# Working-layout inputs and state-space tables kept in DRAM, in a hybrid diffusion block

## The chip, the cores and the metric

The kernel runs on one core of one Trainium2 chip. The metric is the device time of one execution in microseconds. The kernel before was timed in three runs: 2078.35, 2061.95 and 2072.16 us, median 2072.16. Its profile is that of one further execution.

## The reference

One layer of a diffusion backbone, in float32. Tokens: 256 context tokens (`ctx`) and 256 latent tokens (`x`), 2048 channels each. A modulation vector `silu(c) @ w_mod + b_mod` (2048 by 12288, for `c` and for `c_ctx`) gives shifts and scales; `h = x * (1 + scale) + shift` goes through one input projection `w_in` (2048 by 12304), whose columns feed three branches: a Hyena long convolution, a bidirectional mLSTM, and a bidirectional S5 state-space model. The three results are projected, gated, summed and go through `w_out`; then a layer norm, a squared-ReLU feed-forward part (2048 by 8192 and back) and a second layer norm.

What the change touches is mostly the S5 branch. It has 48 groups of 16 channels with 64 complex states each, for two directions:

```
dt = exp(log_dt);  ab = exp(dt * a)            (complex, per group and state)
bb = (ab - 1) / a * b                          (64 x 16 per group)
s[t] = ab * s[t-1] + bb @ u[t]                 (context first, then latent)
y[t] = Re(c @ s[t]);  both directions added, then d * u, gelu and a gated unit
```

## The kernel before

**Streams of weights.** Most of the time TensorE multiplies streamed weights. A chunk of 512 KB is loaded on SyncE's queue into a tile `wr`, split by ScalarE into a high part `wh` (L145) and by VectorE into the rest `wl` (L149), and multiplied in three products per pair of operands (high by high, high by low, low by high; L166, output tile `mm`). One chunk on the latent tokens alone is 24 matmuls of 128x256. Chunks of a column block follow each other over k; between chunks, `chunk_done` (L171) lets side generators advance by a rate. The order of instructions on each engine is then set by a planner, which goes through the traced order as a priority and takes what its own cost model holds to be ready; on the chip every engine runs its list strictly in that order. Tiles come from pools with few buffers, and a pool opened later reuses the memory of a closed one, so its first writers wait for the last readers there.

**First stage, phase 0** (`phase0`, L1476; 0 to about 200 us). For four groups of 512 channels: two blocks of the modulation (`mod_block`, L359, 8 chunks each, matmul L371 on PSUM tile `px`), then `h_load` and `h_group` (L383, L394): the tokens arrive with tokens on partitions, TensorE transposes them (L169, 64 in all), VectorE applies scale and shift (L407) and the result is split (`t`, L145 and L149). Among the next group's chunks run the key columns of the input projection. A side generator, started at the third group at rate 1.5, computes the S5 parameters (`s5_params`, L411: parameter rows are loaded with (direction, pair) on partitions and transposed by TensorE in `expand`), small vectors (`col_load`, `conv_cols`: loaded as rows, transposed, evacuated) and the lag kernels (`s5_lags`, L542: `s5_q`, L527, makes C times the powers of ab with six instructions per direction, forward on VectorE and backward on GpSimd, L535 to L540; 192 small matmul records at L564; result to DRAM as `KK`). At its end the powers and B go to DRAM as `SP`, C and the eighth power as `SC`. All of this lives in the scope `p0a`; its memory is next used by the scope `pA` (keys, values, mLSTM).

**The S5 stage** (scope `pB`, L1582 to L1592; 546 to about 1000 us). `SP` and `SC` have been read back. The stream is 36 chunks of the Hyena columns, then 96 chunks of the gate columns `mg`, of which 32 are traced before the output, 48 beside it, and the rest later. After 6 chunks comes the injection (`s5_inject`, L620): for each of 6 channel tiles, 12 instructions make B times the powers (L645 to L650, half of them on VectorE, half on GpSimd, tiles `s5q`, `z`, `s5tp`), 16 transposes (L169), four evacuations to `z`, 64 matmul records (L663), and evacuations into `S` by ScalarE and VectorE (L668). Then the scan (`s5_scan`, L671, side at rate 2): 63 steps of four GpSimd instructions (L678 to L681) on all of `S`. Then the output (`s5_output`, L684, side at rate 0.6): for each channel tile `s5_q` again makes C times the powers (12 instructions), the states are laid out (`b`, L145 and L707), 32 and 16 matmul records (L714, L720), 16 more to put them in place, and the sum into `z` (L729). `s5_glu` closes the branch.

Of the kernel before, what the change touches and what calls it, by code (L numbers as in the profile page):

```python
# [65 lines left out]

class Tiles(list):
    """Tiles by k, read as one operand [:, k, columns]."""
# [6 lines left out]
class Kern:  # L75
# [15 lines left out]
    # ---------------------------------------------------------------- helpers  # L91
# [4 lines left out]
    def c(self, name, rows=P):  # L96
        o, n = CN[name]
        return self.consts[:rows, o:o + n]

# [25 lines left out]
    def aux(self, shape, tag=None):  # L125
        """A PSUM bank: px for what the stream of weights waits on, aux for side work; in turn where both are free."""
# [44 lines left out]
    def chunk_done(self):  # L171
        """Lets side work be traced between the chunks of the stream of weights."""
# [18 lines left out]
    # weights stationary: out [cols on partitions, tokens]  # L191
    def lin_w(self, w, c0, ncols, kt, xs):
        """A block of columns; returns its PSUM tile [128, slots, 256] and a step function over k."""
# [5 lines left out]
        def step(k0, alone=False):  # L199
            """The products of nk k; with alone, not added to others."""  # L200
# [19 lines left out]
    def lin_w_steps(self, w, c0, ncols, kt, xs, consume):  # L220
        """Yields between the chunks."""
# [51 lines left out]
    def slices(self, buf, view=None, **dims):  # L273
        """Named temporaries out of one tile."""
# [9 lines left out]
    def exp_acc(self, out, x, tmp):  # L284
        """exp in float32 accuracy; tmp(tag, dtype) gives tiles of x's shape."""
# [28 lines left out]
    def rstd(self, var, shape, tag):  # L314
        """1 / sqrt(var + eps)"""
# [11 lines left out]
    def col_load(self, src, n, tag, at=0):  # L327
        """A vector of n*128 in DRAM as columns [128, n]."""
        rows = self.t(self.sm, [96, P], "rows", 2)[:n]
        self.nc.gpsimd.dma_start(rows, src.rearrange("(r p) -> r p", p=P))  # L330
        ps = self.aux([P, n])
        self.tr(ps, rows, n)
        col = self.t(self.cst, [P, n], tag)
        self.act(col, ps)
        return col

    # ---------------------------------------------------------------- phases
    def setup(self):
# [3 lines left out]
        crow = self.t(self.sm, [32, P], "crow", 1)  # L342
        nc.sync.dma_start(crow[:16], I["c"].rearrange("b (r p) -> (b r) p", p=P))
        nc.sync.dma_start(crow[16:], I["c_ctx"].rearrange("(r p) -> r p", p=P))
        ps = self.aux([P, 32])
        self.tr(ps, crow, 32)
        self.sc = self.t(self.cst, [P, 32], "sc")
        self.act(self.sc, ps, AF.Silu)
# [3 lines left out]
        self.bmod = self.col_load(I["b_mod"][0], 96, "bmod")  # L352
        nc.vector.tensor_scalar(self.bmod[:, 16:32], self.bmod[:, 16:32], 1.0, None, op0=ALU.add)
        nc.vector.tensor_scalar(self.bmod[:, 64:80], self.bmod[:, 64:80], 1.0, None, op0=ALU.add)
        self.modc = self.t(self.cst, [P, 32, 2], "modc")
# [27 lines left out]
    def h_load(self, g):  # L383
        nc = self.nc
        raws = []
        for s, src in enumerate((self.I["ctx"][0], self.I["x"][0])):
            src = src[:, g * 512:(g + 1) * 512]
            raw = [self.room[2 * s + tb][:, 4:6, :].rearrange("p k t -> p (k t)") for tb in range(2)]
            for tb in range(2):
                nc.sync.dma_start(raw[tb], src[tb * P:(tb + 1) * P])  # L390
            raws.append(raw)
# [1248 lines left out]
```

## Time and profile before

| what | value |
|---|---|
| median of three runs | 2072.16 us |
| span of the profiled execution | 2066.5 us |
| instructions | 34948 |
| PE busy | 1908.3 us (92%) |
| DVE busy | 1373.0 us (66%) |
| ACT busy | 799.8 us (39%) |
| POOL busy | 526.1 us (25%) |
| DMA moved | 435.64 MB, mean 211 GB/s |

The profile lists the span from the first to the last instruction, 2066.5 us, and no separate total for that execution; the median of the three runs is 5.7 us above it. PE is TensorE, DVE VectorE, ACT ScalarE, POOL GpSimd and SP SyncE, which here only issues loads. Busy PE time is modelled from pipelined instructions, so a stretch with PE at 100% can still go slower than another. The granted clock stands as a share of full speed.

### The profile page before, as it was taken

Reading aid. Unit: us, or ns where it says so; the run is one execution under the profiler, and the core shown is the slowest. Engines: PE = TensorE matmul, PEld = TensorE weight load, DVE = VectorE, ACT = ScalarE, POOL = GpSimd, SP = SyncE. Lnnn points to the kernel's source line nnn. Section 1 sums busy time; section 2 is a strip of 40 time slices with the busy share of each in tenths; the row PEclk is TensorE's granted clock in tenths of the full one; section 3 lists DMA queues with packets and bytes.
Section 4 is the critical chain, followed back from the end, with each engine's and each line's share of the span. In section 5 each row is a group of like instructions: output and inputs, shape, how many; then the busy total and the mean of one; then the engine's idle time right before and its main releaser. Section 6 shows DMA issues by size and latency. Waiting matters only on the chain.

```text
span 2066.5 us, 34948 instructions
## 1 busy us (share of the span) xinstructions
PE 1908.3 (92%) x14085; PEld 1733.0 (84%) x14085; DVE 1373.0 (66%) x1840; ACT 799.8 (39%) x1066; POOL 526.1 (25%) x656
## 2 busy tenths in 40 slices
PE   6889999999888999589988999799999999999995
PEld 2657988989888898579878978799989899998985
DVE  5567877547989855495688766966665555555556
ACT  1323333236444333234433443544443334444331
POOL 3435211000435799960243410500000000000001
PEclk7889999999999999789999999999999999999998
DMA  9777676766666676447766776577776666667663
GB/s 303 244 246 255 200 230 221 228 183 193 219 193 192 209 243 221 130 141 224 265 210 199 263 264 208 178 237 236 231 245 188 191 186 184 183 182 229 192 185 101
DMA packets 243378, 435.64 MB, mean 211 GB/s; under 512 B 22431, under 2 KB 69225, under 8 KB 242225
## 3 DMA queue, kind: packets, MB, share of 16 engines
q1 hardware_dynamic: 221744, 382.29, 59.1%
q0 software_dynamic: 11968, 43.26, 6.2%
q10 hardware_dynamic: 9504, 7.87, 1.4%
q8 instruction: 110, 1.80, 0.4%
q14 instruction: 52, 0.42, 0.1%
HBM read 414.58 MB, written 21.92 MB: 211 GB/s over the span
## 4 chain that ended last, share of the span: by engine, by line
PE 40%; DVE 9%; POOL 8%; DMA 6%; issue 2%; ACT 1%; POOLq 0%; ACTq 0%; DVEq 0%
PE mm L166 39%; DVE wl L149 3%; POOL sc L678 2%; POOL t L681 2%; DMA wr<-in_w_mod_dram 2%; POOL sc L680 2%; DMA wr<-in_w_out_dram 2%; POOL sc L679 2%; ACT wh L145 1%; DVE t L149 1%; DMA wr<-in_w_in_dram 1%; DVE mac L1226 1%; PE aux L166 1%; DMA wr<-in_w_hy_out_dram 1%; DVE b L707 0%
## 5 line engine op out<-in xcount | busy, mean ns | idle before, releaser
L166 PE MATMUL mm<-t,wh 128*128 128x256 f32 x5888 | 1112.5, 289 | 13.2 <-DVE t L149 7.0
L166 PEld LDWEIGHTS mm<-t,wh 128*128 128x128 f32 x5888 | 937.8, 195 | 39.5 <-issue 13.9
L149 DVE TENSOR_TENSOR wl<-wr,wh 128x1024 fp32r<-128x1024 f32 (+1 forms) x517 | 666.0, 1293 | 392.6 <-ACT wh L145 392.1
L145 ACT ACTIVATE wh<-wr 128x1024 fp32r<-128x1024 f32 (+1 forms) x517 | 546.3, 1058 | 841.2 <-PE mm L166 584.5
L166 PE MATMUL mm<-t,wl 128*128 128x256 f32 x2944 | 849.9, 289 | 19.0 <-DVE wl L149 18.8
L166 PEld LDWEIGHTS mm<-t,wl 128*128 128x128 f32 x2944 | 572.7, 195 | 31.5 <-DVE wl L149 23.2
L1226 DVE SCALAR_TENSOR_TENSOR mac<-wr,sc,mac 128x512 f32<-128x512 f32 x240 | 189.7, 790 | 143.6 <-DMA wr<-in_w_mod_dram 141.0
L166 PE MATMUL mm<-wh,t 128*128 128x512 f32 (+1 forms) x960 | 247.5, 347 | 0.0
L166 PEld LDWEIGHTS mm<-wh,t 128*128 128x128 f32 x960 | 168.2, 189 | 23.3 <-ACT wh L145 1.1
L166 PE MATMUL mm<-wl,t 128*128 128x512 f32 (+1 forms) x480 | 168.3, 351 | 5.3 <-DVE wl L149 5.2
L166 PE MATMUL mm<-wh,ff 128*128 128x512 f32 (+1 forms) x576 | 155.3, 358 | 0.0
L166 PEld LDWEIGHTS mm<-wh,ff 128*128 128x128 f32 x576 | 101.8, 188 | 17.6
L166 PEld LDWEIGHTS mm<-wl,t 128*128 128x128 f32 x480 | 90.8, 189 | 22.3 <-DVE wl L149 11.0
L166 PE MATMUL mm<-wl,ff 128*128 128x512 f32 (+1 forms) x288 | 103.0, 357 | 0.0
L1448 POOL DMA_DIRECT2D t<-in_ln_g_dram x1 | 0.5, 532 | 355.9 <-PE mm L166 355.9
L166 PE MATMUL mm<-ty,wh 128*128 128x256 f32 x384 | 73.3, 289 | 0.0
L166 PE MATMUL mm<-ty,wl 128*128 128x256 f32 x192 | 56.7, 296 | 8.5 <-DVE wl L149 8.3
L166 PEld LDWEIGHTS mm<-ty,wh 128*128 128x128 f32 x384 | 60.9, 192 | 0.9
L166 PEld LDWEIGHTS mm<-wl,ff 128*128 128x128 f32 x288 | 54.2, 188 | 8.8
L1237 POOL DMA_DIRECT2D mrow<-b x8 | 4.0, 500 | 224.0 <-DVE b L1235 224.0
L371 PE MATMUL px<-wr,b 128*32 128x512 f32 x128 | 40.6, 723 | 13.5 <-DMA wr<-in_w_mod_dram 13.5
L166 PE MATMUL aux<-t,t 128*128 128x384 f32 (+3 forms) x160 | 47.2, 411 | 5.4 <-DMA t<-HX 1.9
(458 smaller groups left out, 1937.2 us busy)
## 6 DMA issues: line engine op xcount, KB each, us to landing
wr<-in_w_ff_dram SPq DMA_DIRECT2D x256, 512.0 KB, 4.0
wr<-in_w_in_dram SPq DMA_DIRECT2D x192, 512.0 KB, 4.5
wr<-in_w_mod_dram SPq DMA_DIRECT2D x160, 512.0 KB, 4.8
wr<-in_w_out_dram SPq DMA_DIRECT2D x32, 512.0 KB, 4.6
wh<-in_w_mod_dram SPq DMA_DIRECT2D x16, 512.0 KB, 6.0
wl<-in_w_mod_dram SPq DMA_DIRECT2D x16, 512.0 KB, 6.9
MG<-mg POOLq DMA_DIRECT2D x24, 256.0 KB, 4.4
wr<-in_w_ml_out_dram SPq DMA_DIRECT2D x12, 512.0 KB, 4.5
```

The costliest lines, as they stand in the source:

```text
L145: return self.nc.scalar.activation(out, in_, f, bias=bias, scale=scale)
L149: self.nc.vector.tensor_sub(lo, x, hi.bitcast(F32))
L166: self.nc.tensor.matmul(out, lhsT, rhs, start=start, stop=stop, skip_group_check=True)
L371: nc.tensor.matmul(ps[o:o + 32], self.st[:, k, :], raw[:, kk, :], start=k < 4, stop=k >= KT - 4, skip_group_check=True, tile_position=(0, o))
L678: v.tensor_mul(t1, self.a8[:, 0], S[:, :, :, :, n - 1])
L679: v.tensor_mul(t2, self.a8[:, 1], S[:, :, ::-1, :, n - 1])
L680: v.tensor_add(t1, t1, S[:, :, :, :, n])
L681: v.tensor_add(S[:, :, :, :, n], t1, t2)
L1226: v.scalar_tensor_tensor(acc, x, c, acc, op0=ALU.mult, op1=ALU.add)
L1237: nc.gpsimd.dma_start(self.mrow[which // 3:which // 3 + 1, o:o + 512], brow)
L1448: nc.gpsimd.dma_start(g2r, I["ln2_g"].to_broadcast([P, D]))
```

## The change

Some inputs are rearranged on the host without arithmetic (`lay`): the tokens come transposed, channels on partitions; the S5 parameters come with (group of the pair, state) on partitions; all small vectors come as columns of one table `vecs`; the gate columns of `w_in` and the small Hyena weights come packed. On the chip the transposes and evacuations of these inputs go away; the scale and shift now read SBUF and write in place, and the splits are half as many and twice as wide.

The S5 tables are made once. `s5_tables` takes the place of `s5_lags`: for each of 6 channel tiles and 2 halves it makes, per direction, C times the powers for 9 lags (written to DRAM as `QD`, 256 KB each, on GpSimd's queue) and B times the powers for 8 (transposed and written as `WA`, 256 KB each, on ScalarE's queue), with five instructions each (`powers`) in place of six. `QD` and `WA` have 24 writes each. Injection and output read them back, 1 MB per channel tile each, on ScalarE's queue, into two buffers `s5wq`, and have no table arithmetic left; `SP` and `SC` are gone. The side generator starts with the first group of phase 0, at rate 1.0. S5's B and C are loaded at once, without waiting for the first modulation. The scan, the streams and everything behind the S5 stage are as they were.

```diff
+def lay(i):
...
+    ht = np.stack([f("ctx")[0].T, f("x")[0].T]).reshape(2, 4, 4, P, T).transpose(1, 0, 3, 2, 4)
+    gates = f("w_in")[0][:, O_G:O_G + 16].reshape(KT, P, 16).transpose(1, 0, 2)
+    pairs = lambda a: a.reshape(2, 24, 2, 64, -1).transpose(2, 3, 0, 1, 4).reshape(P, 48, -1)
+    dt = np.repeat(f("s5_log_dt")[0][:, :, None], 64, axis=2)
+    s5a = np.stack([pairs(a)[:, :, 0] for a in (f("s5_a_re")[0], f("s5_a_im")[0], dt)], axis=1)
+    s5b = np.stack([pairs(f(n)[0]) for n in ("s5_b_re", "s5_b_im")], axis=1)
+    s5c = np.stack([pairs(f(n)[0].transpose(0, 1, 3, 2)) for n in ("s5_c_re", "s5_c_im")], axis=1)
...
-    def col_load(self, src, n, tag, at=0):
...
+        self.vecs = self.t(self.cst, [P, NVC], "vecs")
+        nc.sync.dma_start(self.vecs, I["vecs"])
+        self.sc = self.vec("sc")
+        self.act(self.sc, self.sc, AF.Silu)
...
-        for s, src in enumerate((self.I["ctx"][0], self.I["x"][0])):
-            src = src[:, g * 512:(g + 1) * 512]
-            raw = [self.room[2 * s + tb][:, 4:6, :].rearrange("p k t -> p (k t)") for tb in range(2)]
-            for tb in range(2):
-                nc.sync.dma_start(raw[tb], src[tb * P:(tb + 1) * P])
+        for s in range(2):
+            raws.append([self.room[2 * s + i][:, 4:6, :] for i in range(2)])
+            for i in range(2):
+                self.nc.sync.dma_start(raws[s][i], self.I["ht"][g, s][:, 2 * i:2 * i + 2, :])
...
-        for j in range(4):
-            k = 4 * g + j
-            ps = self.aux([P, 2, T], "px")
-            for s in range(2):
-                for tb in range(2):
-                    self.tr(ps[:, s, tb * P:(tb + 1) * P], raws[s][tb][:, j * P:(j + 1) * P])
-            h = self.b2([P, 2, T])
+        for i in range(2):
+            k0 = 4 * g + 2 * i
-                m = 1 - s
-                scale, shift = self.modc[:, 16 + k, m:m + 1], self.modc[:, k, m:m + 1]
-                nc.vector.tensor_scalar(h[:, s], ps[:, s], scale, shift, op0=ALU.mult, op1=ALU.add)
-                self.split(hh[:, k, :], hlo[:, k, :], h[:, s])
-
-    # ------------------------------------------------------------- S5
+                h = raws[s][i]
+                for j in range(2):
+                    k, m = k0 + j, 1 - s
+                    self.nc.vector.tensor_scalar(h[:, j], h[:, j], self.modc[:, 16 + k, m:m + 1],
+                                                 self.modc[:, k, m:m + 1], op0=ALU.mult, op1=ALU.add)
+                self.split(hh[:, k0:k0 + 2, :], hlo[:, k0:k0 + 2, :], h)
...
+        nc.gpsimd.dma_start(par, I["s5a"])
+        B, C = (self.t(self.br, [P, 2, 48, 16], tag, 1) for tag in ("s5B", "s5C"))
+        nc.gpsimd.dma_start(B, I["s5b"])
+        nc.gpsimd.dma_start(C, I["s5c"])
...
-        # B and C, [(g2 p), (d pair), c]
-        for name, dst in (("s5_b_re", self.Br), ("s5_b_im", self.Bi), ("s5_c_re", self.Cr), ("s5_c_im", self.Ci)):
-            raw = self.t(self.br, [48, 2048], "s5raw", 2)
-            # not loaded before the first of the modulation is there
-            nc.gpsimd.tensor_copy(raw[:, 0:1], self.modc[:48, 0, 0:1])
-            if name[3] == "b":
-                nc.gpsimd.dma_start(raw, I[name][0].rearrange("d (q g) p c -> (d q) (g p c)", g=2))
-                view = raw.rearrange("r (gp c) -> r c gp", c=16)
-            else:
-                view = raw.rearrange("r (c gp) -> r c gp", c=16)
-                src = I[name][0].rearrange("d (q g) c p -> g (d q) c p", g=2)
-                for g in range(2):
-                    nc.gpsimd.dma_start(view[:, :, 64 * g:64 * g + 64], src[g])
-            yield
-            expand(dst.rearrange("p q c -> p c q"), 16, lambda i: view[:, i, :])
...
+        nc.gpsimd.dma_start(self.A8, a8.rearrange("p a b c d -> p (a b c d)"))
...
+    def powers(self, out, m, d, q, l0, n):
...
+        t = self.work[d][:, :k * 2 * n * 16].rearrange("p (q s l c) -> p q s l c", q=k, s=2, c=16)
+        for s in range(2):
+            bcp = lambda i: pw[:, i].unsqueeze(3).to_broadcast([P, k, n, 16])
+            bcm = lambda i: m[:, i, q, :].unsqueeze(2).to_broadcast([P, k, n, 16])
+            e.tensor_mul(out[:, :, s], bcp(1 + s), bcm(0))
+            e.tensor_mul(t[:, :, s], bcp(s), bcm(1))
+        e.tensor_add(out, out, t)
...
+    def s5_tables(self):
...
+            for half in range(2):
+                for d in range(2):
+                    q = slice(24 * d + 4 * ct + 2 * half, 24 * d + 4 * ct + 2 * half + 2)
+                    Q1 = self.t(self.br, [P, 576], f"s5Q{d}", 1)
+                    Q = Q1.rearrange("p (q s n) -> p q s n", q=2, s=2)
+                    self.powers(Q.rearrange("p q s (l c) -> p q s l c", c=16), self.s5C, d, q, 0, 9)
...
+                    nc.gpsimd.dma_start(self.QD[ct, d, :, 2 * half:2 * half + 2], Q[:, :, :, o:o + P])
+                    yield
+                wt = []
+                for d in range(2):
+                    q = slice(24 * d + 4 * ct + 2 * half, 24 * d + 4 * ct + 2 * half + 2)
+                    w = self.t(self.br, [P, 2, 2, P], "s5w", 4)
+                    self.powers(w.rearrange("p q s (l c) -> p q s l c", c=16), self.s5B, d, q, d, LC)
+                    wt.append(w)
+                for i in range(2):
+                    wa = self.t(self.br, [P, 4, P], "s5wa", 2)
+                    pt = self.aux([P, 4, P])
+                    for d in range(2):
+                        for s in range(2):
+                            self.tr(pt[:, 2 * d + s, :], wt[d][:, i, s])
+                    self.act(wa, pt)
+                    nc.scalar.dma_start(self.WA[ct, :, 2 * half + i], wa)
...
-        self.pieces(cc, self.SC, 1728, 2)
+        a8 = sx[:, 6144:6336]
+        nc.gpsimd.dma_start(a8, self.A8)
...
-                e.tensor_mul(w[:, :, 0], bcp(0), bcb(self.Br))
-                e.tensor_mul(t1, bcp(1), bcb(self.Bi))
-                e.tensor_sub(w[:, :, 0], w[:, :, 0], t1)
-                e.tensor_mul(w[:, :, 1], bcp(0), bcb(self.Bi))
-                e.tensor_mul(t1, bcp(1), bcb(self.Br))
-                e.tensor_add(w[:, :, 1], w[:, :, 1], t1)
...
-            for p in range(4):
-                pt = self.aux([P, 4, P])
-                for d in range(2):
-                    for s in range(2):
-                        self.tr(pt[:, 2 * d + s, :], wt[d][:, p, s].rearrange("p i c -> p (i c)"))
-                wa = spare[:, p % 2].rearrange("p (x m) -> p x m", x=4)
-                self.act(wa, pt)
+            u = self.s5_u(ct, self.t(self.br, [P, 8, P], "s5tp", 2)[:, :, :NCH])
+            wa = self.t(self.br, [P, 4, 4, P], "s5wq", 2)
+            nc.scalar.dma_start(wa, self.WA[ct])
+            for p0 in range(0, 4, 2):
+                pi = self.aux([P, 2, 4, NCH])
+                for i in range(2):
+                    for x in range(4):
+                        for h in range(2):
+                            r = slice(64 * h, 64 * h + 64)
+                            nc.tensor.matmul(pi[r, i, x, :], wa[:, p0 + i, x, r], u[:, 2 * (p0 + i) + h, :],
...
-            Q = [self.t(self.br, [P, 2, 4, P], "s5q", 4) for d in range(2)]
-            for d in range(2):
-                t1 = self.b2([P, 4, LC, 16])
-                self.s5_q(Q[d], t1, ct, d, 1 - d, LC)
-            # chunk-start states
+            Q = self.t(self.br, [P, 2, 4, 2, P], "s5wq", 2)
+            nc.scalar.dma_start(Q.rearrange("p d q s n -> p d (q s n)"),
+                                self.QD[ct].rearrange("d p q s n -> p d (q s n)"))
...
-                    yield from self.s5_lags()
...
+                    yield from self.s5_tables()
+
+                self.with_side(side(), 1.0)
-                    if g == 2:
-                        self.with_side(side(), 1.5)
...
-                # to DRAM, but after the loads that the products wait on
-                k = KT - 4
-                for dst, t in zip((self.SP, self.SC), self.spill):
-                    n = dst.shape[1]
-                    nc.gpsimd.tensor_copy(t[:, n - 1:n], self.modc[:, 16 + k, 0:1])
-                    nc.gpsimd.dma_start(dst, t)
...
-                    keep = self.s5_tiles(pv, "vt")
-                    self.pieces(keep, self.SP, 3264, 4)
```

## Rows read from the trace of the kernel before

**Rows 1.** The chain that ended last, shares of the span by engine.

```profile
PE 40%; DVE 9%; POOL 8%; DMA 6%; issue 2%; ACT 1%; POOLq 0%; ACTq 0%; DVEq 0%
```

**Rows 2.** Stretches: length; busy (count) PE, PEld, DVE, ACT, POOL; PEclk, DMA, GB/s.

```profile
0.00:50.00 50.00, 30.62 (x136) 13.29 (x137) 25.74 (x116) 9.65 (x19) 15.74 (x45) 0.69 0.97 304
50.00:100.00 50.00, 42.41 (x325) 32.45 (x324) 29.86 (x43) 18.28 (x43) 20.91 (x19) 0.84 0.80 248
100.00:150.00 50.00, 42.34 (x317) 28.17 (x315) 31.66 (x42) 12.50 (x35) 17.63 (x17) 0.82 0.71 238
150.00:200.00 50.00, 47.02 (x409) 36.27 (x407) 37.73 (x51) 16.68 (x44) 31.10 (x41) 1.00 0.78 259
...
546.00:702.00 156.00, 137.58 (x1327) 130.87 (x1326) 141.11 (x184) 69.45 (x114) 83.42 (x68) 0.96 0.60 181
702.00:849.00 147.00, 135.45 (x1090) 133.62 (x1089) 85.67 (x78) 52.47 (x56) 138.70 (x211) 0.98 0.72 227
849.00:871.00 22.00, 0.50 (x5) 0.29 (x3) 0.75 (x3) 1.35 (x5) 20.25 (x51) 0.57 0.13 46
871.00:938.00 67.00, 57.07 (x567) 52.47 (x567) 59.30 (x67) 26.38 (x58) 41.02 (x32) 0.86 0.48 148
```

**Rows 3.** PE's timeline, end of the scan: start, length, [idle <-releaser].

```profile
871.12 3.68 PE L714 MATMUL aux<-s5q,b 128*64 128x128 f32 x32 [21.62 <-ACT b L145]
```

**Rows 4.** The scan's tile sc: duration ns min/median/max, first and last start us.

```profile
L678 POOL TENSOR_TENSOR sc<-t x63: 432/444/1476, 702.7 to 870.3; 128x96 f32<-128x96 f32 x63
```

**Rows 5.** Such stretches, tile mm (streamed products) alone: PE, PEld, DVE, ACT.

```profile
546.00:702.00 156.00, 111.74 (x810) 104.57 (x810) 0.00 (x0) 4.68 (x6) 0.96 0.60 181
702.00:849.00 147.00, 134.80 (x1082) 132.79 (x1081) 0.00 (x0) 6.14 (x11) 0.98 0.72 227
...
871.00:938.00 67.00, 23.42 (x175) 22.25 (x175) 0.00 (x0) 1.09 (x2) 0.86 0.48 148
938.00:980.00 42.00, 42.00 (x350) 42.00 (x351) 0.00 (x0) 1.07 (x2) 1.00 0.76 237
```

**Rows 6.** Groups by line, 0:200 us: busy, mean ns | idle before <-releasers.

```profile
L407 DVE TENSOR_SCALAR b<-px,modc 128x256 f32<-128x256 f32 x32 | 15.6, 534 | 2.6 <-PE px L169 2.6
L169 PE MATMUL px<-consts,ty 128*128 128x128 f32 x64 | 13.7, 356 | 6.1 <-DVE modc L380 3.6 <-DVE b L407 2.5
L536 POOL TENSOR_TENSOR s5raw<-s5keep,s5c 128x576 f32<-128x576 f32 x6 | 8.7, 1451 | 0.0
L538 DVE TENSOR_TENSOR s5raw<-s5keep,s5c 128x576 f32<-128x576 f32 x6 | 6.4, 1072 | 0.0
```

**Rows 7.** DMA issues: queue, count, KB each, median us to landing.

```profile
MG<-mg POOLq DMA_DIRECT2D x24, 256.0 KB, 4.4
KD<-KK POOLq DMA_DIRECT2D x8, 384.0 KB, 8.9
rowa<-mrow POOLq DMA_DIRECT2D x2, 1024.0 KB, 7.4
SP<-s5keep POOLq DMA_DIRECT2D x1, 1632.5 KB, 6.2
SC<-s5c POOLq DMA_DIRECT2D x1, 864.5 KB, 10.1
```

**Rows 8.** Who waited for whom, 200:260 us: total, times, longest.

```profile
POOL vt L1549 <- DMA KK<-s5kk: 5.4, 1, 5.4
```

**Rows 9.** ACT's timeline, first use of memory after the first scope.

```profile
212.62 4.35 ACT L145 ACTIVATE t<-ty,mlcb,mlcw 128x512 f32<-128x512 f32 x6
```

**Rows 10.** Stretch 546:702, instructions on tile s5q alone (columns as in rows 2).

```profile
546.00:702.00 156.00, 16.03 (x96) 10.38 (x96) 32.40 (x32) 0.00 (x0) 49.19 (x32) 0.96 0.60 181
```

**Rows 11.** Timeline of PE within the injection: one pair's products, one pair's transposes.

```profile
574.70 0.69 PE L663 MATMUL aux<-s5tp,z 128*64 128x64 f32 x16
575.32 0.66 PE L169 MATMUL aux<-consts,s5q 128*128 128x128 f32 x4
```

**Rows 12.** Groups by line, 546:702 us (columns as in rows 6).

```profile
L145 ACT ACTIVATE t<-aux 128x128 f32<-128x128 f32 x24 | 6.5, 273 | 27.0 <-PE aux L663 27.0
```

More of the change, by code (lines that the diff above doesn't have):

```diff
@@ L98, in c, with vec @@
         return self.consts[:rows, o:o + n]
+    def vec(self, name):
+        o, n = VC[name]
+        return self.vecs[:, o:o + n]
     def t(self, pool, shape, tag, bufs=None, dt=F32):
@@ new lines, in run, with o_consume @@
+            with self.scope("pA") as self.br:
+                self.n6 = 4
+                self.kT, self.kT2 = self.t6([P, 3, 512]), self.t6([P, 3, 512])
+                for i, (acc, step) in enumerate(kparts):
+                    step(12)
+                    self.k_consume(2 * i, 2, acc)
+                n = 2 * HEADS * (DH + 1)
+                vt = self.t(self.br, [P, 2 * n], "vt", 1)
+                self.vt = [vt[:, n * s:n * s + n].rearrange("p (b h d) -> p b h d", b=2, h=HEADS) for s in range(2)]
+                for s in range(2):
+                    nc.gpsimd.memset(self.vt[s][:, :, :, DH:], 1.0)
+                gate = self.t(self.sm, [P, LC], "gate", 1)
+                nc.gpsimd.tensor_copy(gate[:LC], self.kT[:LC, 2, :LC])
+                nc.gpsimd.dma_start(self.KD[:, 0, 0, 0, 0].unsqueeze(1), gate[:LC, 0:1])
+                self.s5_spread()
+                gates = self.gates()
+                next(gates)
+                self.with_side(gates, 0.5)
+                self.with_side(self.mod_late(), 1.75, 1)
+                self.with_side(self.hy_filters(), 1.2, 2)
+                self.lin_w_all(w_in, O_V, W, KT, both, self.v_consume)
+                self.drain()
+                self.qT = self.t6([P, CT, T])
+                self.sides[1][1] = 0.3
+                self.lin_w_all(w_in, O_Q, W, KT, lat, self.q_consume)
+                self.drain(2)
+                self.sides[1][1] = 1.5
+                self.mlstm()
+                self.uT = self.ty()
+                self.lin_w_all(w_in, O_U, W, KT, both, self.u_consume)
+                self.sides[1][1] = 0.6
+                self.oT = self.ty()
+                def o_consume(ct0, nct, ps):
+                    self.act(self.oT[:, ct0:ct0 + nct, :], ps[:, :nct, :])
+                self.lin_w_all(w_in, O_O, W, KT, lat, o_consume)
+                self.mlstm_out()
@@ new lines, in run @@
+            steps = self.lin_w_steps(w_in, O_MG, 3 * D, KT, lat, self.mg_consume)
+            with self.scope("pB") as self.br:
+                self.n6 = 5
+                hy = self.lin_w_steps(w_in, O_HY, 3 * W, KT, lat, self.hy_consume)
+                self.run_steps(hy, 6)
+                self.s5_inject()
+                self.sides[1][1] = 0.3
+                self.with_side(self.s5_scan(), 2)
+                self.run_steps(hy, 36)
+                self.run_steps(steps, 32)
+                self.with_side(self.s5_output(), 0.6)
+                self.run_steps(steps, 48)
+                self.drain()
+                self.s5_glu()
@@ L1631 @@
     given["consts"], given["feats"], given["tabs"] = consts, feats, tabs
+    given.update(lay(inputs))
     for name, a in given.items():
```

352 lines of the change are left out of this document (106 added, 246 removed).

## The prediction

> **What bounds the kernel now.** I read three views, in this order. The chain that ended last says that TensorE's products hold 40% of the span and GpSimd 8% [rows 1]; GpSimd is the surprise, since it is busy 25% of the time and does no streamed work. The table by stretch shows where it sits. Phase 0 (0 to 200 us) is bound by DMA first (share 0.97, 304 GB/s) and then by TensorE and DMA together: PE is busy 42 to 47 of 50 us, at a granted clock of 0.82 to 0.84 for 100 us, with DMA at 0.71 to 0.80 [rows 2]. From 546 to 702 us, the injection, VectorE is the fullest engine (141 of 156 us). From 702 to 849 us GpSimd is (139 of 147): that is the scan. From 849 to 871 us nothing streams: PE's next instruction is the first matmul of the output, and it waits 21.62 us for states [rows 2, 3]. The scan runs from 702.7 to about 873 us, 170 us for 63 steps, and each of its instructions takes 0.44 us when it is undisturbed and up to 1.48 us when not [rows 4].
>
> How far the S5 stage is from TensorE's own need: at full clock a streamed matmul costs 42.00 / 350 = 0.120 us [rows 5]. The 2067 of them in 546 to 938 us need 248 us. What else PE does there is the difference of rows 2 and 5: 25.8 in the injection, 0.7 in the scan, 33.7 in the output, 60 us together. Need 308 us, taken 392: 84 us lost to waits, slow clock and instructions that feed late. That is what the change can reach for; behind 938 us the stream is full again.
>
> **The change, part by part.**
>
> *Token path, phase 0.* Out go 64 transposes (13.7 us of PE busy time, and 6.1 us in which PE idled before them), and 32 scalings from PSUM at 0.534 us become 32 from SBUF; the splits become 16 of double width [rows 6]. No row shows such a scaling from SBUF; I bound it by 0.2 us below and 0.534 above and take 0.4. The S5 parameters lose their 64 transposes, too. PE receives the 96 table transposes, 4 in 0.66 us [rows 11], 16 us. PE's work in phase 0 stays level within 5 us; the gain is the 6 us of idle at most.
>
> *Tables, phase 0.* Per half tile and direction there are now four products of 288 elements, a sum of 576, four products of 256 and a sum of 512. On GpSimd 576 elements cost 1.45 us [rows 6] and 96 cost 0.44 [rows 4], so 2.1 ns an element: 0.85, 1.45, 0.77 and 1.3 us, in all 9.2 us, twelve times 111 us. The lag kernels before took 36 instructions of 1.45, 52 us. On VectorE, at 1.07 us for 576 [rows 6] and about half for half the size, 6.2 us a half tile, 75 us for 39. VectorE was busy 125 of 200 us and GpSimd 85 [rows 2], so both fit. GpSimd also issues 24 writes, some 0.6 us each, and starts near 35 us instead of 72; with waits I get an end near 190 us, where it ended before. Nothing of this is on the path as long as it ends before 212.6 us, when the keys' convolution first writes the memory of that scope [rows 9]; that later writers do wait there is seen in 5.4 us of waiting for the last lag write [rows 8].
>
> *DMA, phase 0.* `WA` and `QD` write 6.29 MB each; `SP` and `SC`, 2.56 MB, go [rows 7]. 10.0 MB more, at 304 / 0.97 = 313 GB/s, is 32 us of full DMA. Free in 50 to 200 us: 50 x (0.20 + 0.29 + 0.22) = 35 us [rows 2]. It fits only if it falls exactly into the gaps, which it will not; the stream's loads, all on SP's queue, land later and TensorE waits for them. Ends: 6 us gained and 32 us lost. I take **10 us lost**, nearer the lower end because the writes are spread over twelve halves while PE, not DMA, is the fuller one after 50 us.
>
> *Injection.* 72 table instructions leave: 24 and 8 of VectorE's take 32.4 us, so 36 take 36 us; GpSimd's 36 take 55 us [rows 10]. 16 us of transposes leave PE. What stays for a channel tile is four times 0.69 us of PE [rows 11], four ScalarE evacuations of 0.27 us [rows 12] and eight smaller ones on VectorE, and what comes is a load of 1 MB, for which the nearest row is 7.4 us to landing [rows 7]. With two buffers the six tiles follow at about 8 us: ready at 546 + 7 + 6 x 8 = 601 us at best, 680 at worst if the injection stays threaded between the 30 Hyena chunks behind it. I take **620 us** for the scan's start, 82 us earlier. ScalarE issues these loads in its own list: one that waits for a buffer holds up the `wh` behind it, and so the stream; at about 8 us of slack per tile I cost that at nothing, and up to 3 us per tile if PE is late.
>
> *Scan and output.* The scan keeps its 63 steps; now it runs beside the Hyena chunks, where VectorE is fuller. Its price is 170 us as measured, or 197 if the excess over 0.44 us grows with VectorE's share (0.64 us mean, from 0.58 of 147 us busy to 0.88). It ends at **790**, or 817 us. Rows 5 hold 1892 products before the output's first matmul, 79 chunks, where the trace order asks for 70; the planner had filled nine more in. With 70, PE gets there after 70 x 24 x 0.120 + 10 = 212 us of need, at the 702 to 849 us pace (147 us for 130 of need, 1.13) 238 us, so at 784: a wait of 6 us is left of the 21.6. The output loses 24 and 16 table instructions from GpSimd and VectorE in a stretch where VectorE is busy 59 of 67 us, and loads 1 MB a tile (7.4 us) under 9.5 us of PE.
>
> *Sum of the S5 stage.* Need 308 - 16 = 292 us, at 1.13 329, plus 6: 335 for 392, **57 us gained**. Ends: 85 (a pace of 1.05) and 25 (the waits return in another place).
>
> *Rest.* Small loads and the packed gate columns stand beside a full PE: nothing. Sum: 2066.5 + 10 - 57 = 2019.5 us of span; with the 5.7 us by which the median of the runs stands above the span, **2025 us**.
>
> **A rule weighed.** Writes of 256 KB from GpSimd's queue land in 4.4 us, and VectorE works throughout that time [rows 7]. The Trainium skill, in "SBUF — State Buffer", section "Who interferes with whom", says that VectorE's two-port modes, among them a `tensor_scalar` from SBUF, keep GpSimd from writing its DMA descriptors; the token scaling becomes such an instruction while `QD` is written. No row here shows a write so held up. By the rule alone `QD` would land later; by the rows it doesn't.
>
> **Rivals.**
>
> *The scan stays the end (20%).* The scan starts late or runs slower, since GpSimd's instructions already go from 0.44 to 1.48 us beside VectorE [rows 4]. Started at 680 and taking 170 it ends at 850, 21 us earlier than now; PE comes at 784, waits, and only those 21 us and some 5 of the output are gained. With 20 lost in phase 0: 2072 - 6 = 2066. For it: the injection's evacuations queue behind VectorE's Hyena work, and the planner's cost model puts instructions too early where GpSimd is slow. Against: VectorE loses 36 us in that very stretch. The same page and section of the Trainium skill has VectorE instructions with two SBUF inputs and GpSimd reads exclude each other; the trace agrees (0.44 against 1.48 us).
>
> *Phase 0 becomes a chain through GpSimd, slower (13%).* The tile of C times the powers has one buffer a direction. If a half tile goes as GpSimd work 9.2, issues 1, then the landing of its write, 8.9 us as for the worst such row [rows 7], then 2 of waiting for PE, it takes 21 us, twelve from 40 us end at 292, 80 us past 212.6, and all behind shifts: 2072 + 80 - 57 = 2095 us. It decides from 212.6 + 57 = 270 us on, 19 us per half. Against: 4.9 us of other products lie between two uses of the buffer, and 4.4 us is the usual landing.
>
> *All of it comes (12%).* Phase 0 gains 6, the S5 stage 80: 1986 us. For it: the clock, 0.86 and 0.57 in 849 to 938 us, returns as PE stays fed.
>
> **How the numbers follow.** The forecast, 2025 us, has 55%; its own range is 1995 to 2048. The range for 8 in 10 reaches over the good end and the unmoved scan: 1985 to 2070. About 1% (21 us) is what a measurement of this kernel can tell from no change. Faster by more: 0.53 of the forecast, 0.12, and 0.02 of the unmoved scan, 0.67. Within: 0.02 and 0.17, 0.19. Slower: 0.13 and 0.01, 0.14.
>
> **What would show it.** Right: the scan's first instruction near 630 us, its last near 800; no idle before the output's first matmul above 10 us; VectorE below 115 of its 156 us where the injection was; the keys' convolution at 215 to 230 us; DMA above 0.85 from 50 to 200 us. Wrong: the last table write after 230 us, TensorE waiting for `WA` or `QD` by several us a tile, or a scan longer than 200 us, each of which hands back what the tables save.

## The result, and the profile after

The changed kernel takes **2039.91 us**, median of four runs (2038.85 to 2046.25), against 2072.05 us for the kernel before in the same session (2061.95 to 2078.35): a ratio of 0.9847, 95% interval 0.9824 to 0.987. The forecast was 2025 us; the result is 15 us above it, inside its own range (1995 to 2048) and the wider one. The profiled execution is the longest of the four, 2046.25 us, with a span of 2044.3 us, so only 1.95 us lie around the span, where I had put 5.7. The two profiled executions are 22.2 us apart and the medians 32.1: the one after is 6.3 us above its median, and the one before, if 1.95 us lie around its span as well, some 3.6 us below (an estimate). So the landmarks below understate the gain by about 10 us; f2, in which phase 0 is unchanged, starts the S5 stage at 575.8 us, so the 6.3 of the changed kernel don't lie in phase 0.

The sum came out near; two of its terms did not. The landmarks of phase 0 come later than in [rows 9], and what follows them is shorter:

| landmark | before | after | step |
|---|---|---|---|
| keys' convolution, first | 212.6 | 228.0 | +15.4 |
| first load of the injection (start of the S5 stage) | 546.1 | 574.6 | +28.4: forecast +10 |
| span less that | 1520.4 | 1469.7 | -50.7: forecast -57 |
| span | 2066.5 | 2044.3 | -22.2: forecast -47 |

The table of stretches after (columns as in [rows 2]):

```profile
0.00:50.00 50.00, 24.73 (x119) 7.31 (x119) 42.44 (x146) 8.70 (x25) 21.15 (x41) 0.83 0.88 314
50.00:100.00 50.00, 38.59 (x267) 28.60 (x269) 37.21 (x45) 15.19 (x42) 38.44 (x47) 0.83 0.79 262
100.00:150.00 50.00, 40.48 (x319) 28.70 (x313) 42.40 (x51) 16.63 (x48) 35.37 (x45) 0.93 0.90 291
150.00:200.00 50.00, 39.74 (x303) 29.16 (x305) 46.35 (x54) 15.86 (x44) 39.01 (x53) 0.90 0.86 289
200.00:250.00 50.00, 40.51 (x321) 37.53 (x312) 44.15 (x77) 20.70 (x35) 17.99 (x24) 0.86 0.63 198
...
546.00:702.00 156.00, 142.76 (x1404) 140.27 (x1403) 103.37 (x192) 69.18 (x110) 70.38 (x111) 0.93 0.82 269
634.00:808.00 174.00, 141.84 (x1122) 139.25 (x1122) 94.73 (x95) 58.05 (x69) 163.62 (x269) 0.92 0.67 215
```

Read the third busy column, VectorE: 168.4 of the first 200 us for 125.0 before. The fifth, GpSimd, is 134.0 for 85.4, and PE fell from 162.4 to 143.5. So in phase 0 VectorE is now the fullest of the five engines and TensorE waits. In 546 to 702 us VectorE fell from 141 to 103 us, as foreseen (below 115).

VectorE's groups by line, 0 to 228 us (columns as in [rows 6]):

```profile
L435 DVE TENSOR_SCALAR ty<-ty,modc 128x256 f32<-128x256 f32 x32 | 21.6, 741 | 0.1
L194 DVE TENSOR_TENSOR wl<-wr,wh 128x1024 fp32r<-128x1024 f32 x13 | 20.4, 1572 | 0.0
L536 DVE TENSOR_TENSOR s5Q<-s5pq,s5C 128x288 f32<-128x288 f32 x24 | 19.2, 838 | 6.1 <-PE aux L564 6.1
L537 DVE TENSOR_TENSOR s5t<-s5pq,s5C 128x288 f32<-128x288 f32 x24 | 18.9, 822 | 0.2
L538 DVE TENSOR_TENSOR s5w<-s5w,s5t 128x512 f32<-128x512 f32 x12 | 17.2, 1430 | 0.3
L536 DVE TENSOR_TENSOR s5w<-s5pq,s5B 128x256 f32<-128x256 f32 x24 | 17.1, 755 | 11.9 <-PE aux L214 11.9
L537 DVE TENSOR_TENSOR s5t<-s5pq,s5B 128x256 f32<-128x256 f32 x24 | 16.2, 716 | 0.3
L194 DVE TENSOR_TENSOR t<-ty,t 128x512 fp32r<-128x512 f32 x16 | 15.7, 1015 | 0.0
L538 DVE TENSOR_TENSOR s5Q<-s5Q,s5t 128x576 f32<-128x576 f32 x12 | 11.7, 972 | 0.2
```

The six table groups sum to 100.3 us (forecast 75), and the scaling's mean is 0.741 us, above even my upper bound of 0.534. The next rows, the two engines' timelines at one moment, show why (start, length; GpSimd first):

```profile
191.25 1.33 POOL L537 TENSOR_TENSOR s5t<-s5pq,s5C 128x288 f32<-128x288 f32 x2
192.53 1.31 POOL L536 TENSOR_TENSOR s5Q<-s5pq,s5C 128x288 f32<-128x288 f32 x2
193.81 1.20 POOL L536 TENSOR_TENSOR s5w<-s5pq,s5B 128x256 f32<-128x256 f32 x2
194.97 1.39 POOL L538 TENSOR_TENSOR s5Q<-s5Q,s5t 128x576 f32<-128x576 f32 x1
196.66 0.78 POOL L568 DMA_DIRECT2D QD<-s5Q  x1 [0.29 <-POOL s5Q L538]
...
191.01 5.91 DVE L538 TENSOR_TENSOR s5w<-s5w,s5t 128x512 f32<-128x512 f32 x1
```

One VectorE sum, whose shortest case is 0.68 us, is held for 5.91 us, until GpSimd has run seven products and sums back to back and turns to issuing a DMA.

In phase 0 of the changed kernel (0 to 228 us) TensorE waited for these: engine, line <- releaser: total, times, longest.

```profile
PE px L406 <- DVE s5t L335: 10.7, 1, 10.7
PE aux L564 <- POOL s5Q L538: 9.5, 4, 4.4
PE mm L211 <- DVE wl L194: 7.8, 6, 3.4
PE mm L211 <- DVE t L194: 5.3, 4, 2.6
PE aux L564 <- issue: 4.8, 1, 4.8
PE aux L564 <- DVE s5Q L538: 4.7, 2, 3.4
PE mm L211 <- ACT t L190: 4.6, 1, 4.6
PE aux L214 <- DVE s5w L538: 4.4, 3, 2.2
...
```

The first is the start of the kernel and is as long in e3 (11.2 us), so it has no part in what follows. The other seven are 41.1 us; for 4.8 of them ("issue") the profile shows nothing that TensorE waited for.

The S5 stage went nearly as foreseen. The scan's tile answers to [rows 4], and the first product of the output to [rows 3]:

```profile
L652 POOL TENSOR_TENSOR sc<-t x63: 433/446/1302, 634.4 to 806.8; 128x96 f32<-128x96 f32 x63
```

```profile
807.68 3.68 PE L687 MATMUL aux<-s5wq,b 128*64 128x128 f32 x32 [15.81 <-POOL sc L652]
```

The scan starts at 634 us (forecast 620) and ends at 808 (790); the output's first matmul still waits, 15.8 us for 21.6. The DMA issues that answer to [rows 7] (queue, count, KB each, median us to landing):

```profile
QD<-s5Q POOLq DMA_DIRECT2D x24, 256.0 KB, 4.9
WA<-s5wa ACTq DMA_DIRECT2D x24, 256.0 KB, 5.2
s5wq<-WA ACTq DMA_DIRECT2D x6, 1024.0 KB, 10.2
s5wq<-QD ACTq DMA_DIRECT2D x6, 1024.0 KB, 7.3
```

The tables' loads take 10.2 and 7.3 us where I had 7.4 for both, and TensorE waits once for one of them, 1.9 us. Of the signs that I named, the scan's two times, VectorE's share in the injection and the convolution's time came; the idle before the output didn't fall to 10 us, and DMA stood at 0.79, 0.90 and 0.86 for "above 0.85". None of the signs of being wrong came: the last table write is at 221.7 us, and the scan takes 174 us.

### The profile page after: what moved, and what is told of

Read it like the earlier page. It is cut to its first block, busy times and chain, and to the rows that moved or that the text cites. A ratio compares the mean times of both kernels' runs of the same rounds, so it can differ in the third digit from the quotient of the medians.

```text
span 2044.3 us, 34693 instructions
## 1 busy us (share of the span) xinstructions
PE 1885.0 (92%) x13945; PEld 1716.5 (84%) x13945; DVE 1342.6 (66%) x1842; ACT 797.7 (39%) x1079; POOL 473.4 (23%) x654
## 4 chain that ended last, share of the span: by engine, by line
PE 64%; DVE 14%; DMA 8%; POOL 8%; issue 4%; ACT 1%; ACTq 0%; POOLq 0%; DVEq 0%; SPq 0%
PE mm L211 57%; DMA wr<-in_w_mod_dram 4%; PE aux L211 4%; DVE wl L194 4%; POOL sc L654 2%; POOL sc L653 2%; POOL t L655 2%; POOL sc L652 2%; DVE t L194 1%; DMA wr<-in_w_in_dram 1%; DVE ty L435 1%; ACT wh L190 1%; DVE mac L1181 1%; DVE s5t L537 1%; DMA s5wq<-WA 1%
## 5 line engine op out<-in xcount | busy, mean ns | idle before, releaser
L194 DVE TENSOR_TENSOR wl<-wr,wh 128x1024 fp32r<-128x1024 f32 (+1 forms) x517 | 657.0, 1277 | 381.6 <-ACT wh L190 380.7
L1181 DVE SCALAR_TENSOR_TENSOR mac<-wr,vecs,mac 128x512 f32<-128x512 f32 x240 | 186.8, 778 | 152.7 <-DMA wr<-in_w_mod_dram 150.0
L211 PEld LDWEIGHTS mm<-wh,ff 128*128 128x128 f32 x576 | 101.8, 188 | 17.6
L211 PEld LDWEIGHTS mm<-wl,t 128*128 128x128 f32 x480 | 91.6, 191 | 21.7 <-DVE wl L194 10.5
L406 PE MATMUL px<-wr,b 128*32 128x512 f32 x128 | 40.3, 714 | 12.9 <-DVE s5t L335 10.7
```

The source lines that it names most:

```text
L194: self.nc.vector.tensor_sub(lo, x, hi.bitcast(F32))
L211: self.nc.tensor.matmul(out, lhsT, rhs, start=start, stop=stop, skip_group_check=True)
L406: nc.tensor.matmul(ps[o:o + 32], self.st[:, k, :], raw[:, kk, :], start=k < 4, stop=k >= KT - 4, skip_group_check=True, tile_position=(0, o))
L1181: v.scalar_tensor_tensor(acc, x, c, acc, op0=ALU.mult, op1=ALU.add)
```

## The experiments

Theories for the 28 us lost in phase 0 (for the 10 that I expected): **A**, VectorE is held up by the table products on both engines; **B**, the written bytes; **C**, TensorE meets the tables too early in its own order; **D**, the chain of tables on GpSimd itself. Every edit can shift the planner's order elsewhere, so I go by landmarks beside the totals. Ratios are to the kernel before (2074.4 to 2074.7 us in these runs, 2072.05 for the first row).

| kernel | median us | ratio, 95% | keys' conv. | injection's first load | wait before output |
|---|---|---|---|---|---|
| after | 2039.9 | 0.9847 [0.9824, 0.987] | 228.0 | 574.6 | 15.8 |
| e1 first tile's tables written | 2032.4 | 0.9799 [0.9771, 0.9828] | 221.9 | 568.2 | 17.6 |
| e2 first tile's products made | 2017.0 | 0.9721 [0.9699, 0.9742] | 206.1 | 551.7 | 20.4 |
| e3 all products on VectorE | 2003.8 | 0.9659 [0.9641, 0.9676] | 200.8 | 542.8 | 19.0 |
| e4 TensorE's part later | 2040.4 | 0.9838 [0.9818, 0.9858] | 227.2 | 575.1 | 19.6 |
| e5 e3, scan on VectorE | 1979.2 | 0.9539 [0.9503, 0.9576] | 199.0 | 540.8 | 0.3 |
| e6 e3, scaling on ScalarE | 2010.3 | 0.97 [0.9667, 0.9734] | 203.0 | 549.5 | 21.3 |
| e7 before, new token path | 2069.8 | 0.9977 [0.9953, 1.0001] | 213.2 | 548.2 | 22.0 |
| e8 GpSimd's products alone | 2027.8 | 0.9783 [0.9749, 0.9816] | 231.4 | 566.1 | 20.8 |
| f1 e3, first tile's tables written | 2006.6 | 0.9672 [0.966, 0.9685] | 201.1 | 542.1 | 21.8 |
| f2 after, scan on VectorE | 2011.8 | 0.9701 [0.9688, 0.9714] | 229.5 | 575.8 | 0.6 |
| f3 before, lag kernels on VectorE | 2061.9 | 0.9939 [0.9925, 0.9953] | 190.7 | 537.1 | 22.2 |
| f4 e5, products of four pairs | 1989.9 | 0.9589 [0.9569, 0.9609] | 195.0 | 542.7 | 1.6 |

**e1, the bytes.**

```diff
+                    if ct == 0:
+                        nc.gpsimd.dma_start(self.QD[ct, d, :, 2 * half:2 * half + 2], Q[:, :, :, o:o + P])
...
+                    if ct == 0:
+                        nc.scalar.dma_start(self.WA[ct, :, 2 * half + i], wa)
...
-            nc.scalar.dma_start(wa, self.WA[ct])
+            nc.scalar.dma_start(wa, self.WA[0])
```

> Tables of the first channel tile alone are written to DRAM, and injection and output read this one for all six (their numbers are then not the reference's); the table arithmetic, TensorE's part of it and all reads stay. 10.5 MB of writes and 40 DMA issues of ScalarE and GpSimd leave phase 0. Changed kernel: 2039.9 us, key convolution from 228.0 us, first load of the injection at 574.6 (546.1 before the change). Theory B, the 28 us lost in phase 0 are DMA bytes: the key convolution comes at 205 to 215 us, 2012 to 2022 us in all. Theory A, they are VectorE held up by table arithmetic, and theory C, they are TensorE waiting in its own order for tables: no more than 5 us gained, 2035 to 2040 us.

It gained 7.5 us: more than A and C allowed, far from B. Whether the 7.5 are bytes or the 20 issues on GpSimd, at 0.78 us each, this run doesn't say; f1 prices both where GpSimd has no table products.

**e2, the products.** `powers` is called under `if ct == 0`, for both tables; the other tiles use what is there.

> The table products (powers) are made for the first channel tile alone; the tiles of this one are then multiplied, transposed, evacuated and written for all six (numbers are not the reference's). 200 of 240 table instructions leave VectorE and GpSimd; bytes, TensorE's and ScalarE's part stay. Theories A (VectorE held up) and C (TensorE waits in order for tables): the key convolution comes at 200 to 210 us and the time falls to 2010 to 2022 us. Theory B (DMA bytes): 2035 to 2040 us.

22.9 us gained, as A and C expected; D fits as well. It isn't clean: with the data there at once, all 24 `QD` writes are issued by 74 us, and TensorE is busy 36.6 of 50 to 100 us beside DMA at 0.93. So it weighs less than e3, which has all the arithmetic.

**e3, GpSimd out of the tables.**

```diff
-        e = self.nc.vector if d == 0 else self.nc.gpsimd
+        e = self.nc.vector
```

> Both directions' table products on VectorE, none on GpSimd. In the changed kernel VectorE's 288- and 256-element products have a mean of 0.72 to 0.84 us against a shortest of 0.41 to 0.45, its sums 0.97 and 1.43 against 0.75 and 0.68. Theory A1, the two engines hold each other up: all products go to their shortest, 116 us for both directions where VectorE's alone now take 100, the splits get shorter as well, and the time stays within 10 us of 2040 on either side. Theory A2, VectorE is simply full whatever GpSimd does: 100 us more of VectorE work in phase 0, the key convolution at 270 us or later, 2080 to 2140 us.

36.1 us gained: A2 is gone, and A1, which expected no more than 10, expected too little. The groups of VectorE in this run, 0 to 197 us:

```profile
L536 DVE TENSOR_TENSOR s5Q<-s5pq,s5C 128x288 f32<-128x288 f32 x48 | 19.8, 453 | 1.3 <-DMA QD<-s5Q 1.2
L537 DVE TENSOR_TENSOR s5t<-s5pq,s5C 128x288 f32<-128x288 f32 x48 | 19.3, 451 | 0.0
L537 DVE TENSOR_TENSOR s5t<-s5pq,s5B 128x256 f32<-128x256 f32 x48 | 17.7, 417 | 0.0
L536 DVE TENSOR_TENSOR s5w<-s5pq,s5B 128x256 f32<-128x256 f32 x48 | 17.5, 419 | 7.3 <-PE aux L214 7.3
L538 DVE TENSOR_TENSOR s5Q<-s5Q,s5t 128x576 f32<-128x576 f32 x24 | 17.5, 751 | 0.0
L538 DVE TENSOR_TENSOR s5w<-s5w,s5t 128x512 f32<-128x512 f32 x24 | 16.1, 684 | 0.1
L194 DVE TENSOR_TENSOR wl<-wr,wh 128x1024 fp32r<-128x1024 f32 x12 | 14.6, 1218 | 2.6 <-ACT wh L190 2.6
L435 DVE TENSOR_SCALAR ty<-ty,modc 128x256 f32<-128x256 f32 x32 | 11.1, 410 | 0.0
L194 DVE TENSOR_TENSOR t<-ty,t 128x512 fp32r<-128x512 f32 x16 | 10.5, 681 | 0.0
```

Twice the products in 107.9 us, where half of them took 100.3. And the first 200 us of the changed kernel, of e3 and of e8 (columns as in [rows 2]):

```profile
0.00:200.00 200.00, 143.54 (x1000) 93.76 (x1002) 168.40 (x294) 56.38 (x158) 133.97 (x184) 0.87 0.86 289
```

```profile
0.00:200.00 200.00, 159.09 (x1138) 107.46 (x1139) 172.16 (x445) 65.18 (x177) 34.13 (x80) 0.89 0.94 322
```

```profile
0.00:200.00 200.00, 148.45 (x1009) 95.85 (x1010) 96.38 (x218) 59.85 (x161) 122.69 (x180) 0.87 0.88 300
```

VectorE is as busy in e3 as in the changed kernel, with 151 instructions more and 100 us of GpSimd's time gone; PE gets 15.6 us more done. A busy engine was a waiting engine.

**e8, the other half.** Here VectorE's products are left out after the first channel tile (`if ct == 0 or d == 1`), GpSimd's stay.

> The changed kernel (2039.9 us) with GpSimd's table products all made and VectorE's made for the first channel tile alone (its tiles serve all six; numbers are not the reference's). Theory A1, VectorE and GpSimd hold each other up, and VectorE's lateness is what costs: GpSimd's products go towards their shortest (0.61 to 0.68 us for a product, 94 us in all for 113), VectorE's splits to 1.22, and 15 to 25 us are gained: 2015 to 2025 us. Theory D, GpSimd's own chain of tables is what ends phase 0: it gains the shortening alone, 5 to 15 us, and the last table write stays at 195 us or later: 2025 to 2035 us.

12.1 us gained, as D expected. VectorE is busy 96 us of 200 (third row above), GpSimd's last `KK` write comes at 224 us, and TensorE waits 8.3 us for GpSimd's `s5Q`. So emptying VectorE gives a third of what e3 gives by filling it: GpSimd in the tables is what costs. It does so by holding VectorE up (A; the token scalings still take 0.758 us in the mean here, for 0.410 in e3) and by being late itself (D). How the 36 us divide between the two stays open.

**e4, the order.** The lag products were traced after the next B tables, the transposes after the next half's C tables:

```diff
+                if late is not None:
+                    self.late_w(*late)
...
+                self.late_q(pk, half, qq, qs)
+                late = (ct, half, wt)
```

> The same work; TensorE's lag products are traced after the next tables (B times powers) and the transposes for WA after the next half's C times powers, so that TensorE meets them later in its order. Theory C: of the 26 us in which TensorE waits for a table or its sum in phase 0 some 15 to 25 go, key convolution at 205 to 213 us, 2015 to 2025 us. Theory A: TensorE then waits for the splits instead, 2036 to 2044 us.

No change; TensorE's wait for GpSimd's `s5Q` is 10.4 us for 9.5. Moving the consumer by one step didn't help while the producer was late. C falls in this form.

**f1, the bytes without the hold-up.** e1's edit on e3.

> e3 (all table products on VectorE, 2003.8 us) with the tables of the first channel tile alone written and read for all six (numbers are not the reference's): 10.5 MB of writes and 40 DMA issues leave phase 0, where DMA was at 0.91 to 0.97. My term of 10 us for these bytes: 1991 to 1997 us. Full DMA all the way, 32 us for them: 1970 to 1980 us. Writes that fall into gaps: 2000 to 2004 us.

Nothing gained (2006.6 for 2003.8), though DMA falls from 0.94 and 0.91 to 0.76 and 0.60 in 100 to 200 us. My 10 us for the bytes are not found: in e3 they fall into gaps. B as the cause of the 28 us is gone; in the changed kernel itself the writes with their issues are worth no more than e1's 7.5 us.

**e7, the token path by itself.** `h_load` and `h_group` of the change in the kernel before.

> The kernel before (2074.5 us in these runs) with the token path of the change alone: tokens loaded transposed, scaled from SBUF in place, split in double width; S5 parameters, lag kernels and the S5 stage as before. My step gives it at most 6 us: 2068 to 2073 us. The rival, that scaling from SBUF beside GpSimd costs 0.7 us in place of 0.4 and eats it up: 2073 to 2078 us.

The total is 5 us lower, as the step had it, and the interval just touches no change. But the mechanism is the rival's. The scalings from SBUF, in 0 to 200 us of this run:

```profile
L400 DVE TENSOR_SCALAR ty<-ty,modc 128x256 f32<-128x256 f32 x32 | 22.6, 777 | 0.1
```

They take 0.777 us, where those from PSUM took 0.534, and phase 0 is no shorter: the keys' convolution comes at 213.2 us (212.6 before), the injection's first load at 548.2 (546.1). Where the 5 us come from, if they are there, stays open.

**f3, the kernel before.**

```diff
-        e = self.nc.vector if d == 0 else self.nc.gpsimd
+        e = self.nc.vector if d == 0 or n == 9 else self.nc.gpsimd
```

> The kernel before (2074.7 us) with the backward lag kernels' 36 products of 576 elements on VectorE in place of GpSimd, nothing else moved: 36 x 0.75 = 27 us more of VectorE work in phase 0, 52 us less of GpSimd's. If the two engines hold each other up in the kernel before, too, VectorE's products of 576 go from their mean of about 1.07 to 0.75 us (12 us back on 36) and the splits shorten: 2066 to 2074 us. If the kernel before had little of it, since its lag kernels start at 65 us only and GpSimd is busy a third of the time: 2072 to 2082 us.

12.5 us gained, more than expected: the kernel before had the same trouble. TensorE waited 0.2 us in all for GpSimd's lag products there, so little of the 12.5 can be TensorE waiting for a late GpSimd (D). VectorE's splits, by tile up to 205 and 212 us (min/median/max ns), in f3 and then in the kernel before:

```profile
L149 DVE TENSOR_TENSOR wl<-wr,wh x15: 1209/1218/1226, 46.0 to 204.6; 128x1024 fp32r<-128x1024 f32 x15
```

```profile
L149 DVE TENSOR_TENSOR wl<-wr,wh x15: 1217/1222/2787, 45.9 to 210.9; 128x1024 fp32r<-128x1024 f32 x15
```

**e6, VectorE relieved.**

```diff
-                    self.nc.vector.tensor_scalar(h[:, j], h[:, j], self.modc[:, 16 + k, m:m + 1],
-                                                 self.modc[:, k, m:m + 1], op0=ALU.mult, op1=ALU.add)
+                    self.act(h[:, j], h[:, j], AF.Identity, bias=self.modc[:, k, m:m + 1],
+                             scale=self.modc[:, 16 + k, m:m + 1])
```

> As e3 (2003.8 us), with the 32 token scalings on ScalarE (busy 17 to 19 of 50 us in phase 0) in place of VectorE. Theory A, a VectorE that is full at 42 to 45 of 50 us is the bound of phase 0: 13 us of it go, the key convolution some 5 to 10 us earlier, 1994 to 2000 us. Rival: the last group's scaling, split and products are a chain in which ScalarE's 0.4 to 0.5 us come in place of VectorE's 0.41, and DMA at 0.91 to 0.97 is the bound by now: 2001 to 2007 us.

6.5 us slower, worse than the rival's range: TensorE waits 10.3 us for ScalarE's `t`, for 1.5 in e3. ScalarE already makes the high parts; the scaling lengthens that chain.

**e5 and f2, the scan.**

```diff
     def s5_scan(self):
 
-        v = self.nc.gpsimd
+        v = self.nc.vector
```

> Both directions' tables on VectorE as in e3 (2003.8 us), and the scan's 252 instructions on VectorE as well. In e3 the scan takes 174 us on GpSimd (599 to 773) and TensorE waits 19.0 us for its end. Theory: the scan's end still holds the output's first matmul, and each step is four instructions of some 0.2 to 0.3 us on VectorE, which is busy 30 of 50 us there: the scan ends before TensorE comes to the output, the 19 us go, 1980 to 1992 us. Rival: 63 steps interleaved with splits of 1.2 us put the splits late and TensorE waits for them: 2000 to 2020 us.

> The changed kernel (2039.9 us) with the scan's instructions on VectorE and all else as it is. Phase 0 stays as it is (first load of the injection at 570 to 578 us). Theory, the scan's end holds the output and GpSimd's scan holds VectorE up: the 15.8 us of TensorE's wait go, and some 5 us more as in e5 against e3 (24.6 us in all): 2014 to 2024 us. Rival, that without e3's earlier start TensorE meets another wait in its place: 2030 to 2040 us.

24.6 us gained on e3 and 28.1 on the changed kernel, each a little more than the theory's range. So the two moves nearly add up: 36.1 and 28.1 alone, 60.7 together. The wait before the output is 0.3 and 0.6 us. Of the other 12 us in f2, some 8 are streamed products that TensorE got done before that wait would begin. Tile `mm` alone, in the changed kernel and then in f2 (columns as in [rows 5]):

```profile
634.00:792.00 158.00, 139.81 (x1098) 136.40 (x1096) 0.00 (x0) 5.88 (x10) 0.95 0.73 234
```

```profile
634.00:792.00 158.00, 145.74 (x1165) 142.80 (x1164) 0.00 (x0) 6.94 (x12) 0.98 0.77 244
```

These are 67 products more, at the 0.120 us of [rows 5]. Another 1.7 us are the output's first 32 matmuls: 3.68 us after the wait, at a granted clock of 0.50 (the lower level, 1.2 GHz) once TensorE had done nothing for 15.6 us, and 1.97 us in f2, at 1.00 (2.4 GHz). The rest I didn't place. The changed kernel's weight split in the scan's stretch (634 to 808 us; its stretch is the last row of the first table above):

```profile
L194 DVE TENSOR_TENSOR wl<-wr,wh 128x1024 fp32r<-128x1024 f32 x45 | 63.4, 1433 | 20.0 <-ACT wh L190 20.0
```

f2's stretch, then its groups:

```profile
634.00:808.00 174.00, 162.45 (x1365) 159.08 (x1363) 154.88 (x358) 71.77 (x93) 11.88 (x20) 0.98 0.78 253
```

```profile
L194 DVE TENSOR_TENSOR wl<-wr,wh 128x1024 fp32r<-128x1024 f32 x51 | 62.1, 1218 | 0.2 <-ACT wh L190 0.2
...
L652 DVE TENSOR_TENSOR sc<-t 128x96 f32<-128x96 f32 x61 | 20.2, 331 | 1.4
```

VectorE goes from 95 to 155 us of 174, and PE from 142 to 162 all the same (15.8 of these 20 are the wait): the splits are 1.22 us again, and the scan's instructions take 0.33 us for GpSimd's 0.39 to 0.43 at best. **e5, both moves, is the fastest version that was run: 1979.2 us, 4.6% below the kernel before and 3.0% below the change.**

**f4, wider instructions.** `powers` for four pairs at a time.

> e5 (1979.2 us) with the table products made for four pairs at a time in place of two: 120 VectorE instructions in place of 240, products of 576 and 512 elements at about 0.75 and 0.68 us in place of two at 0.45 and 0.42, so some 15 to 18 us less of VectorE work in phase 0, and half as many QD writes of twice the size. If VectorE (42 to 45 of 50 us) is still the bound there: 1966 to 1974 us. If DMA (0.86 to 0.98) is by now: 1975 to 1982 us.

10.7 us slower than e5, a miss for both. (The profiled execution of e5 is its shortest, 8 us below its median, that of f4 1.8 above.) Phase 0 is no shorter (the injection's first load at 542.7 for 540.8), so fewer and wider VectorE instructions bring nothing there; but the loss lies behind phase 0: the output's first sum into `z` comes at 774.8 us for 766.1, in code that the edit doesn't touch. What delays it I didn't find.

## Why the prediction was near in total, and wrong in phase 0

**The step that failed is the tables' cost in phase 0**: "On VectorE ... 75 us", and "so both fit". For an undisturbed engine the 75 us were more than enough: e3 has 107.9 us for both directions, 54 for one. (My 1.07 us for 576 elements was itself the mean of products beside GpSimd; f3 has 0.75.) But the change lays GpSimd's products over VectorE's from 24 to 213 us, and beside each other VectorE's half takes 100.3 us. Scaling, splits and tables together lost 67 us of VectorE's time to that: 46 in the tables (100.3 - 54), 10.6 in the scaling (32 x (741 - 410) ns), 4.6 and 5.3 in the splits of weights and tokens. I added two columns of busy time as if the engines were independent, though [rows 4] had shown that they are not, and I had used it against the scan alone.

**The DMA term**, 10 us lost, went the right way for the wrong reason. In f1 the bytes cost nothing. The 28 us that were lost come from GpSimd's tables: with its products on VectorE the S5 stage starts at 542.8 us, 3 earlier than in the kernel before. That is still 5.7 us later than in f3, the kernel before with its lag kernels on VectorE. And here luck helped the total: without the 10 us for bytes the forecast would have been 2015 us, 25 off in place of 15.

**Token path**: a gain of at most 6 us; alone (e7) 5 at the edge of no change, and none of it in phase 0's landmarks. I took 0.4 us a scaling, which is right when undisturbed (0.410 in e3), but it was 0.741 in the change and 0.777 in e7. From PSUM it had not been exposed: the scalings of the kernel before, by tile (min/median/max ns), keep their length beside a GpSimd that is busy 85.4 of 200 us.

```profile
L407 DVE TENSOR_SCALAR b<-px,modc x32: 528/532/544, 45.0 to 189.5; 128x256 f32<-128x256 f32 x32
```

**The rule weighed.** For phase 0 I read of its section the clause on descriptors alone. `QD` lands after 4.9 us in the median in the changed kernel, and 6.3 in e3 without GpSimd's table products, so the medians give no sign of writes held up by the scaling. The clause that fits what happened is beside it, and I had taken it for the scan only: the Trainium skill, "SBUF — State Buffer", section "Who interferes with whom", says that a VectorE instruction with two SBUF inputs contends with GpSimd instructions that read SBUF, and that copies and `tensor_scalar` can contend, too. The trace agrees: sums of 0.68 us take up to 5.91, the scaling from SBUF 0.40 to 2.39, and the one from PSUM stays at 0.53 to 0.54.

**Injection, scan, output**: 57 us forecast, 50.7 found between two single executions that, as said above, understate the gain by some 10. The scan began 14 us later than forecast, since the stage began 28 later and the injection was faster (60 us from first load to scan for 74). **The first rival**, that the scan stays the end, had part of the mechanism: the scan did not start late, at 680, but TensorE waited 15.8 us for its end where I left 6, and f2 prices the scan on GpSimd at 28.1 us. **The second**, a chain through GpSimd past 212.6 us, came in part: the last table write is issued at 221.7 us, not at 292, and the keys' convolution waited 3.1 us for such a write.

**Around the span**: 1.95 us, not 5.7. The difference of a median and one profiled span isn't a property of the kernel.

**The whole miss**: 18.4 us in phase 0 and 6.3 in the S5 stage, less 3.8 around the span and less the 6.3 by which the profiled execution is above its median: 14.6 us.

## What to carry to other kernels

Before two engines are given halves of a job, look whether each one's instructions keep their shortest length while the other works: min against mean in the same group shows it, and busy time of a held-up engine counts its waiting. Here VectorE alone did all the tables in about the time that it needed for half of them beside GpSimd (107.9 and 100.3 us), and it did the scan beside its splits in 162 us, where GpSimd took 174 for the scan alone. Moving the consumer one step didn't help against a late producer (e4), and leaving out bytes that fit into gaps won nothing (f1).

## What was not expected of the hardware

- A single VectorE instruction was held across seven GpSimd instructions in a row (5.91 us for 0.68), not for one at a time.
- An in-place `tensor_scalar` from SBUF took 0.40 to 2.39 us beside GpSimd's products and 0.40 to 0.58 without them (e3); read from PSUM it stayed within 0.53 to 0.54.
- 10.5 MB more of writes in 200 us, with DMA at 0.94, made no difference in time (2003.8 with, 2006.6 without: e3 and f1).
